# Decays one chunk ahead in four buffers, a pad ahead of the projections' input, and matmuls of 512 + 256 columns

## The chip, the cores and the metric

The kernel runs on one core of a Trainium2 chip. The metric is the time of one execution on the device in microseconds, the median of several runs. TensorE multiplies matrices, VectorE (DVE), ScalarE (ACT) and GpSimd (POOL) work element by element, SyncE (SP) issues loads. Each has a queue of its own, in which instructions run in their order; semaphores tie the queues together. SBUF is the memory on the core with 128 partitions, PSUM holds the results of matmuls.

## The reference

One encoder block over 1024 tokens of width 1024: a combined projection, a gated DeltaNet of 4 heads (convolution, decay, chunks, both directions), an mLSTM of 4 heads, an output projection, and PEER, which picks 16 of 128 x 128 single-neuron experts for each token and head. Cut to what the change touches:

```python
p = _rmsnorm(x, norm1_g[l]) @ w_in[l]          # (gq, gk, gv, gz, ga, gb, mq, mk, mv, mo, mi, mf)
qkv = silu(_conv_centred(concat([gq, gk, gv]), conv_w))
qh, kh = _l2norm(q) * DK ** -0.5, _l2norm(k)
# chunked delta rule, per direction
g = jnp.cumsum(g, axis=-1)
decay = jnp.exp(jnp.where(incl, g[..., :, None] - g[..., None, :], -jnp.inf))
a_mat = jnp.where(strict, jnp.einsum("bhncd,bhnsd->bhncs", k_beta, k) * decay, 0.0)
t_mat = lax.linalg.triangular_solve(eye + a_mat, eye, left_side=True, lower=True)
qk = jnp.where(incl, jnp.einsum("bhncd,bhnsd->bhncs", q, k) * decay, 0.0)
...
x = x + concat([y_a, y_b], -1) @ w_out[l]
h2 = _rmsnorm(x, norm2_g[l])
scores = jnp.einsum("thpd,hpkd->thpk", h2 @ w_q, sub_keys)        # router: queries, then keys
act = jax.nn.gelu(jnp.einsum("td,thkd->thk", tb, u_tab[idx]), approximate=False)
x = x + jnp.einsum("thk,thkd->td", gate * act, v_tab[idx])
```

## The kernel before

The program is one stream of about 47,700 instructions in five stages. The front part (0 to about 530 us) normalises, projects and prepares both mixers; the triangular levels, the delta rule and the mLSTM follow to 735; the output projection to 860; then the router and the experts' activations to about 2300, and the experts' output to the end.

**Projections.** `hTh` and `hTl` are the normalised input, transposed, as a high and a low part in a format for fast matmuls (fp32r); each weight is split alike (`split_w`: load `wraw`, high part `whi` by a cast on ScalarE at L120, low part `wlo` by a subtraction on GpSimd at L121). `mm3` (L128) adds three products (high-high, high-low, low-high) over 8 slices: one group of 24 matmuls makes 128 output columns for 512 tokens in a PSUM tile `psP`, of which there are four. 66 such groups, 1584 matmuls, make the whole projection.

**Convolution.** `conv_tile` (L400) projects one of 8 key/query tiles, convolves it on VectorE and applies Silu on ScalarE. The loop behind it takes each tile in two halves: transposes (`psR`), Square, sum and Sqrt for the norm, product, transposes back (`psB`, L440), and a copy by ScalarE into `kT` or `qT` (L441); there are 16 such copies.

**Decay stage.** `amat(n)` handles chunk n of 8 in both directions d, so there are 16 units. It multiplies keys with keys (`pkk`, L452) and keys with queries (`pqk`, L455). A unit loads two tiles of 256 KB, repeated for all partitions, on SyncE's queue (`dec` and `bb`, L387); GpSimd adds a mask (L459); four Exps follow on ScalarE (L462); GpSimd multiplies (L463); VectorE multiplies `bb` by `pkk` (L464) and `dec` by `pqk` (L469). ScalarE's queue issues six stores: `atsc` (L465), four small `dinv` (L468) and `qksc` (L470). `dec` and `bb` have three buffers each (`APB`) in a pool `ap` on the right side of SBUF. `invert` (L480) reads `dinv` of four chunks and inverts 32 x 32 blocks on VectorE in 31 steps.

**mLSTM keys and queries.** 16 groups of projections fill `mkT` and `mqT` (L513 to L520); ScalarE copies them out of `psP`. Their pool `mp` is opened behind the decay stage's in the text. Then come values and gates (`plain`, `value_rows`), 24 groups more.

**Order.** A scheduler arranges the instructions on each engine by its own timeline; the order of the text is the priority. A tile that takes the place of an older one waits for all that used it. `tc.issue_after(ins)` keeps the instructions inside it behind `ins`.

**Experts.** `act_steps` (L1087) multiplies 128 experts' rows by 768 tokens (`TB`), twice 384 columns (`HB`), with the same three products over 8 slices; there are 128 tiles, 6144 matmuls. The router's queries (psq) take `w` = 384 columns in the same manner.

Of the kernel before, what the change touches and what calls it, by code (L numbers as in the profile page):

```python
# [8 lines left out]
F32 = mybir.dt.float32  # L9
# [5 lines left out]
AF = mybir.ActivationFunctionType  # L15
OP = mybir.AluOpType
PSUM = bass.MemoryType.PSUM

P = 128
# [3 lines left out]
NT = S // P  # L23
NH = 4
# [18 lines left out]
GRING, KRING, RING = 6, 4, 6  # L43
WB, VX = 8, 2
LAG = 8
APB = 3
NBUF = 3
AHEAD = 1
EPS = 1e-6
# [13 lines left out]
def kernel(ctx, tc, x, norm1_g, w_in, conv_w, gdn_a_log, gdn_dt_bias, gdn_norm_g,  # L63
# [85 lines left out]

    st_c = ExitStack()  # L150
    csp = pool(st_c, "csp", side="right")
    negm = csp.tile([P, 2, P], F32, name="negm")
    lvl = csp.tile([P, 2, 2, P // 2], F32, name="lvl")
    ones = csp.tile([P, P], F32, name="ones")
# [238 lines left out]
    def unit(d, h, n):  # L393
        return d * 32 + h * NT + n
# [21 lines left out]
    def to_rows(cv, q):  # L416
# [2 lines left out]
            T.transpose(ps[:, j], cv[:, (4 * q + j) * P:(4 * q + j + 1) * P], ident)  # L419
        return ps  # L420

    for ty, dst in ((1, kT), (0, qT)):
        for h in range(NH):
            cv = conv_tile(ty * NH + h)
            for q in range(2):
                ps = to_rows(cv, q)
                rows = wx.tile([P, 4, P], F32, name="rows", bufs=2)
                A.activation(rows, ps, AF.Square)
                ss = wp.tile([P, 4], F32, name="ss", bufs=2)
                V.tensor_reduce(ss, rows, axis=AX, op=OP.add)  # L430
                A.activation(ss, ss, AF.Sqrt, bias=epsc)
                V.reciprocal(ss, ss)
                if ty == 0:
                    V.tensor_scalar(ss, ss, HD ** -0.5, None, op0=OP.mult)
                V.tensor_tensor(rows, ps, ss[:, :, None].to_broadcast([P, 4, P]), op=OP.mult)
                if ty == 1:
                    dmas(ksc[4 * q:4 * q + 4, :, h].rearrange("n p e -> p n e"), rows)
                pb = px.tile([P, 4, P], F32, name="psB", tag="px")
                for j in range(4):
                    T.transpose(pb[:, j], rows[:, j], ident)  # L440
                A.copy(dst[:, h, q * 512:(q + 1) * 512].rearrange("p (a b) -> p a b", b=P), pb)  # L441


    st_b = ExitStack()
    ap_ = pool(st_b, "ap", side="right")
    HALF = NT // 2

    def amat(n):
        cs = slice(n * P, n * P + P)
        pkk = px.tile([P, NH, P], F32, name="pkk", tag="px")  # L450
        for h in range(NH):
            T.matmul(pkk[:, h], kT[:, h, cs], kT[:, h, cs], start=True, stop=True)  # L452
        pqk = px.tile([P, NH, P], F32, name="pqk", tag="px")
        for h in range(NH):
            T.matmul(pqk[:, h], kT[:, h, cs], qT[:, h, cs], start=True, stop=True)  # L455
        for d in range(2):
            dec = rows_bcast(ap_, 0, d, n, "dec", bufs=APB)
            bb = rows_bcast(ap_, 1, d, n, "bb", bufs=APB)
            G.tensor_tensor(dec, dec, negm[:, d:d + 1].to_broadcast([P, NH, P]), op=OP.add)  # L459
            for h in range(NH):  # L460
                u = unit(d, h, n)
                A.activation(dec[:, h], dec[:, h], AF.Exp, bias=gcol[:, J_NG, u:u + 1])  # L462
            G.tensor_tensor(bb, dec, bb, op=OP.mult)  # L463
            V.tensor_tensor(bb, pkk, bb, op=OP.mult)  # L464
            dmas(atsc[d, n], bb)  # L465
            for b in range(4):
                sl = slice(32 * b, 32 * b + 32)
                dmas(dinv[d, n, :, b].rearrange("h s c -> s h c"), bb[sl, :, sl])  # L468
            V.tensor_tensor(dec, pqk, dec, op=OP.mult)  # L469
            dmas(qksc[d, n], dec)  # L470


# [27 lines left out]
        dmas(blocks_of(yinv, 0, half), Y[fw].rearrange("p s c -> p (s c)"))  # L500
        dmas(blocks_of(yinv, 1, half), pq[bw])

    for half in range(2):
        for n in range(half * HALF, half * HALF + HALF):
            amat(n)
        invert(half)
    st_b.close()
    st_a.close()

# [266 lines left out]

    h2sc = scratch("h2sc", [S, D])
    TB = NB * P
    HB = TB // 2
    pg = pool(ctx, "pg")  # L780
    h2Th = pg.tile([P, KD, TB], F32R, name="h2Th")
    h2Tl = pg.tile([P, KD, TB], F32R, name="h2Tl")
# [96 lines left out]
    def router_topk(blocks, hh, hl, between, gate, keep):  # L879
# [6 lines left out]
        off_c = wo.tile([P, TOPK, n], BF16, name="off_c")  # L886
        dof_c = wo.tile([P, TOPK, n], BF16, name="dof_c")
        io_c = wo.tile([P, TOPK, n], BF16, name="io_c")
        nh = 2 if nt > 512 else 1
        w = nt // nh  # L890

        def top16(src, m, vv, ii):
            V.max(vv[:, 0:8], src)
# [6 lines left out]
        def scores(h):  # L900
            sc = wo.tile([P, nb, 2, NK], F32, name="sc", bufs=1)
            for p in range(2):
# [3 lines left out]
                kyT = wo.tile([P, NK], F32, name="kyT", bufs=2)  # L906
                dma(kyT, keys[hp])
                qy = wo.tile([P, nt], F32, name="qy", bufs=2)
                for half in range(nh):
                    ps = psK.tile([P, 512], F32, name="psq")  # L910
                    sl = slice(half * w, half * w + w)
                    mm3(ps[:, :w], lambda k: wh[:, k], lambda k: wl[:, k],
                        lambda k: hh[:, k, sl], lambda k: hl[:, k, sl], KD)
                    A.copy(qy[:, sl], ps[:, :w])
# [165 lines left out]

    def act_steps(uh, ul, psA):

        pa = psA.tile([P, 2, 512], F32, name="pa")
        for k in range(KD):
            for m, (a, b) in enumerate(((uh, h2Th), (uh, h2Tl), (ul, h2Th))):
                for half in range(2):
                    T.matmul(pa[:, half, :HB], a[:, k], b[:, k, half * HB:half * HB + HB],  # L1087
                             start=(k == 0 and m == 0), stop=(k == KD - 1 and m == 2))
            if k < KD - 1:
                yield None  # L1090
        ge = de.tile([P, TB], F32, name="ge", bufs=2)
        A.activation(ge.rearrange("p (a b) -> p a b", b=HB), pa[:, :, :HB], AF.Gelu)
        yield ge

    def act_tile(uh, ul, psA):
# [258 lines left out]
```

## Time and profile before

| | us |
|---|---|
| median of 3 runs | 3323.37 (3322.82 to 3323.91) |
| the profiled execution | 3328.18 |
| its span | 3326.4 |
| TensorE busy | 3170.6 (95% of the span) |
| VectorE busy | 2250.3 |
| GpSimd busy | 1611.2 |
| ScalarE busy | 1224.3 |
| mean granted TensorE clock | 0.977 of full speed |

The profiled execution's own time lies 4.8 us above the median, 0.14%. A row of the chain of waits is the piece of work that ended last at its time; a row of a timeline is an instruction or a run of equal ones, and in brackets the idle time ahead of it and who ended it. "PE" is TensorE. A small unlabelled "q" behind an engine (ACTq) is its queue issuing a transfer.

### The profile page before, as it was taken

How to read it: one execution, taken by the hardware profiler on the slowest of the kernel's cores; microseconds unless marked ns; L12 is line 12 of the kernel's file. 1: busy time of each engine (PE TensorE's matmuls, PEld its weight loads, DVE VectorE, ACT ScalarE, POOL GpSimd, SP SyncE). 2: the span in 40 equal slices, each digit the busy share in tenths (PEclk: the TensorE clock that was granted, in tenths of full speed). 3: DMA queues.
4: the chain of work that ended last, by engine and by line, in shares of the span. 5: the costliest groups of instructions: out<-in, count | busy, mean ns of one | idle time of the engine just before them, and what ended most of it. 6: DMA issues, size and time to landing. Idle time of an engine off the chain costs nothing.

```text
span 3326.4 us, 47752 instructions
## 1 busy us (share of the span) xinstructions
PE 3170.6 (95%) x17106; PEld 2883.3 (87%) x17106; DVE 2250.3 (68%) x5058; ACT 1224.3 (37%) x2223; POOL 1611.2 (48%) x1187
## 2 busy tenths in 40 slices
PE   7798789989999999989999999998999999999998
PEld 6686678987899999989999999996888888888887
DVE  5441682576667767866666666667888775988784
ACT  5443433324323233436566566542222122221211
POOL 1223323442088888886666666643443331453340
PEclk9898999999999999999999999999999999999999
DMA  3216635877545445657988988889999876998882
GB/s 102 71 51 146 172 91 182 250 224 239 176 92 103 85 93 109 144 131 249 316 277 294 320 292 289 310 288 374 355 326 322 306 273 213 372 339 314 283 298 98
DMA packets 486398, 745.86 MB, mean 224 GB/s; under 512 B 106928, under 2 KB 328560, under 8 KB 485392
## 3 DMA queue, kind: packets, MB, share of 16 engines
q1 hardware_dynamic: 279152, 335.68, 32.0%
q0 software_dynamic: 129024, 268.69, 26.8%
q10 hardware_dynamic: 77984, 138.43, 11.3%
q8 instruction: 135, 2.21, 0.3%
q14 instruction: 103, 0.84, 0.1%
HBM read 603.82 MB, written 138.84 MB: 223 GB/s over the span
## 4 chain that ended last, share of the span: by engine, by line
PE 79%; DMA 8%; DVE 7%; issue 2%; ACT 2%; POOL 1%; ACTq 0%; SPq 0%; DVEq 0%; POOLq 0%
PE pa L1087 29%; PE po L1282 15%; PE held L1282 15%; PE psq L128 5%; PE psP L128 5%; PE psg L1208 3%; PE psO L128 2%; DVE pq L496 1%; DMA dinv<-bb 1%; DVE cv L411 1%; PE pss L920 1%; DMA Wt<-rowb 1%; DMA dec<-rowb 1%; DVE Yd L498 1%; DMA qksc<-dec 1%
## 5 line engine op out<-in xcount | busy, mean ns | idle before, releaser
L1121 POOL DMA_INDIRECT gd<-gateB,idxB x384 | 646.9, 1685 | 194.4 <-issue 111.9
L1022 POOL DMA_INDIRECT g<-in_peer_v_dram,idxA x256 | 352.8, 1378 | 515.2 <-DVE ac L1047 375.1
L1087 PE MATMUL pa<-h2Th,uh 128*128 128x384 f32 x2048 | 557.8, 353 | 0.0
L1087 PE MATMUL pa<-h2Th,ul 128*128 128x384 f32 x2048 | 525.9, 337 | 0.2 <-DVE ul L1078 0.2
L1087 PE MATMUL pa<-h2Tl,uh 128*128 128x384 f32 x2048 | 523.6, 336 | 0.0
L1022 POOL DMA_INDIRECT g<-in_peer_u_dram,idxA x256 | 350.6, 1370 | 332.7 <-DVE act L1031 266.1
L1087 PEld LDWEIGHTS pa<-h2Th,ul 128*128 128x128 f32 x2048 | 372.0, 188 | 0.5 <-DVE ul L1078 0.5
L1087 PEld LDWEIGHTS pa<-h2Tl,uh 128*128 128x128 f32 x2048 | 370.9, 188 | 0.0
L1252 ACT CAST wh<-g 128x768 fp32r<-128x768 f32 x128 | 106.7, 834 | 689.6 <-PE po L1282 599.0
L1087 PEld LDWEIGHTS pa<-h2Th,uh 128*128 128x128 f32 x2048 | 349.1, 190 | 0.0
L1047 DVE SCALAR_TENSOR_TENSOR ac<-g,act,ac 128x1024 f32<-128x1024 f32 x254 | 324.6, 1278 | 6.9 <-DMA g<-in_peer_v_dram,idxA 5.6
L1031 DVE CUSTOM_DVE_ANT_0 g<-g,h2A 128x1024 f32<-128x1024 f32 x256 | 305.6, 1218 | 21.1 <-DMA g<-in_peer_u_dram,idxA 21.1
L1203 DVE TENSOR_SCALAR at<-iotr,iT,gT 128x128 f32<-128x128 f32 x384 | 133.0, 365 | 220.4 <-PE psg L1208 220.2
L1282 PE MATMUL held<-h2Tl,wh 128*128 128x512 f32 x576 | 223.0, 389 | 1.5 <-DVE h2Tl L1261 1.5
L1282 PE MATMUL po<-h2Th,wh 128*128 128x512 f32 x576 | 224.1, 389 | 0.0
L1282 PE MATMUL po<-h2Tl,wh 128*128 128x512 f32 x576 | 224.1, 389 | 0.0
L1282 PE MATMUL po<-h2Th,wl 128*128 128x512 f32 x576 | 224.1, 389 | 0.0
L1282 PE MATMUL held<-h2Th,wl 128*128 128x512 f32 x576 | 222.0, 389 | 0.0
L1282 PE MATMUL held<-h2Th,wh 128*128 128x512 f32 x576 | 219.8, 389 | 0.9 <-ACT h2Th L1260 0.9
L1077 ACT CAST uh<-g 128x1024 fp32r<-128x1024 f32 x128 | 134.3, 1049 | 215.1 <-PE pa L1087 212.9
L1291 DVE TENSOR_TENSOR oacc<-po,oacc 128x512 f32<-128x512 f32 x186 | 127.4, 685 | 124.8 <-PE po L1282 124.4
L128 PE MATMUL psP<-hTh,whi 128*128 128x512 f32 x512 | 206.8, 404 | 2.5 <-ACT whi L120 2.5
(389 smaller groups left out, 6710.6 us busy)
## 6 DMA issues: line engine op xcount, KB each, us to landing
g<-in_u_t_dram SPq DMA_DIRECT2D x128, 512.0 KB
g<-in_peer_v_dram SPq DMA_DIRECT2D x128, 512.0 KB
gesc<-ge ACTq DMA_DIRECT2D x128, 384.0 KB
g<-gesc SPq DMA_DIRECT2D x128, 384.0 KB
gd<-zero ACTq DMA_DIRECT2D x24, 1024.0 KB
go<-stage ACTq DMA_DIRECT2D x6, 4096.0 KB
gt<-go SPq DMA_DIRECT2D x64, 384.0 KB
gt<-gd SPq DMA_DIRECT2D x192, 128.0 KB
```

Source lines behind the costliest of these rows:

```text
L128: T.matmul(ps, a(i), b(i), start=(k == 0), stop=(k == 3 * nk - 1))
L1022: tc.keep_in_program_order(G.indirect_dma_start(out=g, out_offset=None, in_=tab, in_offset=bass.IndirectOffsetOnAxis(ap=idxA[:, b, k // TO ...
L1031: V.tensor_tensor_reduce(out=g, in0=g, in1=h2A, op0=OP.mult, op1=OP.add, scale=1.0, scalar=0.0, accum_out=acts[b][:, k:k + 1])
L1047: V.scalar_tensor_tensor(accs[b], g, w, accs[b], op0=OP.mult, op1=OP.add)
L1077: last_act.append(A.copy(uh, ur).ins)
L1087: T.matmul(pa[:, half, :HB], a[:, k], b[:, k, half * HB:half * HB + HB], start=(k == 0 and m == 0), stop=(k == KD - 1 and m == 2))
L1121: tc.keep_in_program_order(G.indirect_dma_start(out=gd[b], out_offset=bass.IndirectOffsetOnAxis(ap=idxB[:, b, h, k:k + 1], axis=0), in_=ga ...
L1203: V.tensor_scalar(at, iotr, iT[:, t:t + 1], gT[:, t:t + 1], op0=OP.is_equal, op1=OP.mult)
L1208: mms.append(T.matmul(ps[:, j], bt, at, start=True, stop=True).ins)
L1252: last_act.append(A.copy(wh, ge).ins)
L1282: T.matmul(po, a[:, tl], b[:, cl], start=(m == 0 and (q == 0 or not mine)), stop=(m == last and (q == NG - 1 or not mine)))
L1291: V.tensor_tensor(dst, po, dst, op=OP.add)
```

## The change

Three things change.

1. **A pad.** `csp.tile([P, 48])` takes 192 bytes of each partition ahead of the other tiles of that side. The built programs place `hTh` at byte 158144 before and 157952 after, `hTl` at 190912 and 190720: before 192 bytes past a multiple of 256, now on one. The other tiles that TensorE reads as its moving operand stand on such multiples in both.
2. **The decay stage.** Loads, mask, Exps and GpSimd's product go into `decays(n)`, which is called one chunk ahead of `amat(n, decs)`. `dec` and `bb` have four buffers. The Exps stand behind the twelfth of the 16 copies into `kT`/`qT`. VectorE makes all four products of a chunk before the stores are issued.
3. **Columns.** The 768 tokens of an act tile, and of the router's queries, are cut into 512 + 256 instead of 384 + 384. The number of matmuls stays.

```diff
-APB = 3
+APB = 4
...
     csp = pool(st_c, "csp", side="right")
+    csp.tile([P, 48], F32, name="pad")
...
+    laid = []
...
-                A.copy(dst[:, h, q * 512:(q + 1) * 512].rearrange("p (a b) -> p a b", b=P), pb)
+                laid.append(A.copy(dst[:, h, q * 512:(q + 1) * 512].rearrange("p (a b) -> p a b", b=P), pb).ins)
...
-    def amat(n):
+    def decays(n):
+
+        out = []
+        for d in range(2):
+            dec = rows_bcast(ap_, 0, d, n, "dec", bufs=APB)
+            bb = rows_bcast(ap_, 1, d, n, "bb", bufs=APB)
+            G.tensor_tensor(dec, dec, negm[:, d:d + 1].to_broadcast([P, NH, P]), op=OP.add)
+            with tc.issue_after(laid[11]):
+                for h in range(NH):
+                    u = unit(d, h, n)
+                    A.activation(dec[:, h], dec[:, h], AF.Exp, bias=gcol[:, J_NG, u:u + 1])
+            G.tensor_tensor(bb, dec, bb, op=OP.mult)
+            out.append((dec, bb))
+        return out
+
+    def amat(n, decs):
...
-            G.tensor_tensor(bb, dec, bb, op=OP.mult)
+        for dec, bb in decs:
             V.tensor_tensor(bb, pkk, bb, op=OP.mult)
+            V.tensor_tensor(dec, pqk, dec, op=OP.mult)
+        for d, (dec, bb) in enumerate(decs):
             dmas(atsc[d, n], bb)
...
-            V.tensor_tensor(dec, pqk, dec, op=OP.mult)
             dmas(qksc[d, n], dec)
...
-    for half in range(2):
-        for n in range(half * HALF, half * HALF + HALF):
-            amat(n)
-        invert(half)
+    ready = decays(0)
+    for n in range(NT):
+        decs = ready
+        if n + 1 < NT:
+            ready = decays(n + 1)
+        amat(n, decs)
+        if n % HALF == HALF - 1:
+            invert(n // HALF)
...
-    HB = TB // 2
+    PARTS = [slice(c, min(c + 512, TB)) for c in range(0, TB, 512)]
...
-        pa = psA.tile([P, 2, 512], F32, name="pa")
+        pa = psA.tile([P, 1024], F32, name="pa")
...
-                for half in range(2):
-                    T.matmul(pa[:, half, :HB], a[:, k], b[:, k, half * HB:half * HB + HB],
+                for sl in PARTS:
+                    T.matmul(pa[:, sl], a[:, k], b[:, k, sl],
```

Lines of the changed kernel are one higher from L151 on, and fifteen higher behind the decay stage.

The pool `ap` fills its side of SBUF downwards. Its lowest buffer begins at byte 84352 of a partition before, at 80064 now (a buffer each of `dec` and `bb`, 2048 bytes, and the pad less). `mkT` takes bytes 67328 to 83712 in both, so two buffers of `dec` now lie on its place.

The scheduler's order on ScalarE, before, among the convolution's copies (`rows` and `ss` belong to the norm of one half, `whi` is the high part of a weight):

```order
L520 ACTIVATE mkT_1888<-psP_1895 128x512 [waits PE_49]
L441 COPY kT_403<-psB_921 128x512 [waits PE_49]
L428 ACTIVATE rows_932<-psR_927 128x512 [waits DMAHW0_49,PE_49]
L431 ACTIVATE ss_934<-ss_934,epsc_59 128x4 [waits DVE_49]
L120 CAST whi_2007<-wraw_2005 128x1024 [waits DMAHW7_49,PE_49,Pool_49]
L520 ACTIVATE mkT_1888<-psP_1921 128x512 [waits PE_49]
```

And now, at the end of the decay stage (`qksc` is the last store of the last unit, `DMAHW1` the lane that reports its landing):

```order
L480 DMA dinv<-bb_1750 32x4x32 [waits DMAHW0_49]
L481 DMA qksc<-dec_1748 128x512 [waits DMAHW1_49,DVE_49]
L535 ACTIVATE mkT_1889<-psP_1896 128x512 [waits DMAHW1_49]
L535 ACTIVATE mkT_1889<-psP_1922 128x512
L535 ACTIVATE mkT_1889<-psP_1954 128x512
L535 ACTIVATE mkT_1889<-psP_1980 128x512
L535 ACTIVATE mkT_1889<-psP_2012 128x512 [waits PE_49]
```

The first copy into `mkT` stood ahead of half of the copies into `kT`; it now stands behind the last store of the stage, with the copies of all four `psP` tiles in a row.

On TensorE, before, in the decay stage (a piece of a group of projections, a chunk's two products, the next piece):

```order
L128 MATMUL psP_2421<-hTh_130,whi_2416 128x512 [waits Activation_49]
L128 MATMUL psP_2421<-hTl_131,whi_2416 128x512
L128 MATMUL psP_2447<-hTh_130,whi_2416 128x512
L128 MATMUL psP_2447<-hTl_131,whi_2416 128x512
L452 MATMUL pkk_1506<-kT_403 128x128 [waits DVE_49,PE_49]
L452 MATMUL pkk_1506<-kT_403 128x128 x3
L455 MATMUL pqk_1511<-qT_402,kT_403 128x128 [waits DVE_49,PE_49]
L455 MATMUL pqk_1511<-qT_402,kT_403 128x128 x3
L128 MATMUL psP_2421<-hTh_130,wlo_2417 128x512 [waits Pool_49]
```

And now, over the stage's last two chunks (the six chunks before stand right ahead of them in the same manner):

```order
L469 MATMUL pkk_1758<-kT_404 128x128 [waits DVE_49,PE_49]
L469 MATMUL pkk_1758<-kT_404 128x128 x3
L472 MATMUL pqk_1763<-qT_403,kT_404 128x128 [waits DVE_49,PE_49]
L472 MATMUL pqk_1763<-qT_403,kT_404 128x128 x3
L469 MATMUL pkk_1784<-kT_404 128x128 [waits DVE_49,PE_49]
L469 MATMUL pkk_1784<-kT_404 128x128 x3
L472 MATMUL pqk_1789<-qT_403,kT_404 128x128 [waits DVE_49,PE_49]
L472 MATMUL pqk_1789<-qT_403,kT_404 128x128 x3
L128 MATMUL psP_2012<-hTh_131,whi_2008 128x512 [waits Activation_49]
L128 MATMUL psP_2012<-hTl_132,whi_2008 128x512
L128 MATMUL psP_2012<-hTh_131,wlo_2009 128x512 [waits Pool_49]
```

No projection stands between the chunks' products any more; 528 of the 1584 stand ahead of the first `pkk` (811 before), and the fifth `psP` tile comes behind the last chunk. Ahead of the first `pkk` there are, behind the last of those 528, only the transposes of seven halves of the convolution.

On GpSimd, before, at the first units (`negm` is the mask):

```order
L459 TENSOR_TENSOR dec_1378<-dec_1378,negm_69 128x512 [waits DMAHW3_49,DMAHW4_49,DMAHW2_49,DMAHW5_49,DMAHW0_49,DVE_49]
L459 TENSOR_TENSOR dec_1396<-dec_1396,negm_69 128x512 [waits DMAHW7_49,DMAHW3_49]
L463 TENSOR_TENSOR bb_1380<-dec_1378,bb_1380 128x512 [waits DVE_49,DMAHW2_49,Activation_49,Pool_49]
L459 TENSOR_TENSOR dec_1424<-dec_1424,negm_69 128x512 [waits DMAHW6_49,DMAHW5_49]
L463 TENSOR_TENSOR bb_1398<-dec_1396,bb_1398 128x512 [waits DVE_49,DMAHW4_49,PE_49,DMAHW6_49,Activation_49,Pool_49]
L121 TENSOR_TENSOR wlo_1053<-wraw_1050,whi_1052 128x1024 [waits DMAHW1_49,PE_49,Activation_49]
```

And now:

```order
L456 TENSOR_TENSOR dec_1369<-dec_1369,negm_70 128x512 [waits DMAHW0_49,DVE_49]
L456 TENSOR_TENSOR dec_1379<-dec_1379,negm_70 128x512 [waits DMAHW4_49,DMAHW5_49,DMAHW3_49,DMAHW6_49,DMAHW2_49,DVE_49]
L456 TENSOR_TENSOR dec_1389<-dec_1389,negm_70 128x512 [waits DMAHW5_49]
L456 TENSOR_TENSOR dec_1399<-dec_1399,negm_70 128x512 [waits DMAHW0_49]
L121 TENSOR_TENSOR wlo_1054<-wraw_1051,whi_1053 128x1024 [waits DMAHW1_49,PE_49,Activation_49]
```

Four additions instead of three stand ahead of the sixth weight tile's low part, and the products `bb` have moved behind it (they follow four weight tiles later).

## Rows read from the trace of the kernel before

**Rows 1.** Table of stretches: busy time (and instructions) of each engine.

```profile
core 0: us, PE busy (x) PEld busy (x) DVE busy (x) ACT busy (x) POOL busy (x), PEclk, DMA share, GB/s
20.00:130.00 110.00, 83.34 (x350) 66.42 (x350) 44.79 (x76) 47.50 (x81) 22.87 (x12) 0.88 0.29 67
...
262.00:400.00 138.00, 105.09 (x491) 86.70 (x491) 61.26 (x93) 56.63 (x97) 51.18 (x33) 0.88 0.69 166
400.00:530.00 130.00, 118.55 (x564) 97.88 (x562) 81.14 (x99) 39.99 (x56) 30.38 (x23) 0.96 0.39 108
...
860.00:2305.00 1445.00, 1414.19 (x8498) 1404.06 (x8498) 994.58 (x3170) 667.05 (x1328) 995.50 (x693) 0.99 0.72 217
2305.00:3326.00 1021.00, 1010.64 (x4458) 836.25 (x4456) 802.96 (x1015) 222.12 (x266) 358.07 (x252) 1.00 0.82 293
```

**Rows 2.** Chain of waits, 90 to 262 us: start, us, what.

```profile
98.20 5.79 DMA dec<-rowb
...
104.12 1.29 POOL dec L459
...
117.75 2.16 POOL dec L459
...
126.94 1.12 PE psB L440 x4
...
137.44 0.44 PE psB L440 x4
...
215.50 12.15 PE psP L128 x53
```

**Rows 3.** Waits, 262 to 400 us: total us, times, longest.

```profile
DVE bb L464 <- POOL bb L463: 68.4, 9, 19.9
POOL dec L459 <- DMA dec<-rowb: 48.0, 6, 20.5
```

**Rows 4.** Chain of waits at the end of the projections.

```profile
523.25 5.36 PE psP L128 x23
```

**Rows 5.** Chain of waits of the whole span: output projection, act tile, router queries.

```profile
805.28 10.90 PE psO L128 x48
...
940.80 29.15 PE pa L1087 x168
...
1361.23 5.75 PE psq L128 x48
```

**Rows 6.** Timeline of GpSimd, 84 to 131 us.

```profile
121.64 2.34 POOL L121 TENSOR_TENSOR wlo<-wraw,whi 128x1024 fp32r<-128x1024 f32 x1 [0.51 <-ACT whi L120]
```

**Rows 7.** Timeline of VectorE: the sum in one half of the convolution.

```profile
254.79 0.69 DVE L430 TENSOR_REDUCE ss<-rows 128x4 f32<-128x512 f32 x1 [6.39 <-ACT rows L428]
```

**Rows 8.** Timeline of ScalarE: the copy of the same half.

```profile
262.12 0.59 ACT L441 COPY qT<-psB 128x512 f32<-128x512 f32 x1 [4.19 <-PE psB L440]
```

**Rows 9.** Chain of waits of the whole span, 262 to 320 us.

```profile
274.84 2.40 DMA dinv<-bb
...
294.54 8.98 DMA atsc<-bb
...
313.45 9.09 DMA dec<-rowb
```

**Rows 10.** SyncE's DMA queue, 314 to 322 us: packets, MB, share of 16 engines.

```profile
q1 hardware_dynamic: 1122, 0.56, 78.7%
```

**Rows 11.** Timeline of ScalarE, 262 to 300 us.

```profile
264.18 1.92 ACTq L468 DMA_DIRECT2D dinv<-bb  x4
...
270.08 5.14 ACTq L468 DMA_DIRECT2D dinv<-bb  x4
...
277.44 1.28 ACT L462 ACTIVATE dec<-dec,gcol 128x128 f32<-128x128 f32 x4
```

**Rows 12.** Timeline of VectorE: products of the first two units and the last.

```profile
263.08 1.29 DVE L464 TENSOR_TENSOR bb<-pkk,bb 128x512 f32<-128x512 f32 x2 [6.06 <-PE pkk L452]
...
394.21 0.69 DVE L464 TENSOR_TENSOR bb<-pkk,bb 128x512 f32<-128x512 f32 x1
```

More of the change, by code (lines that the diff above doesn't have):

```diff
@@ L455, in amat @@
             T.matmul(pqk[:, h], kT[:, h, cs], qT[:, h, cs], start=True, stop=True)
[L456 to L462, printed above, removed]
-            G.tensor_tensor(bb, dec, bb, op=OP.mult)
+        for dec, bb in decs:
             V.tensor_tensor(bb, pkk, bb, op=OP.mult)
+            V.tensor_tensor(dec, pqk, dec, op=OP.mult)
+        for d, (dec, bb) in enumerate(decs):
             dmas(atsc[d, n], bb)
@@ L888, in router_topk @@
         io_c = wo.tile([P, TOPK, n], BF16, name="io_c")
-        nh = 2 if nt > 512 else 1
-        w = nt // nh
         def top16(src, m, vv, ii):
@@ L908, in scores @@
                 qy = wo.tile([P, nt], F32, name="qy", bufs=2)
-                for half in range(nh):
+                for c in range(0, nt, 512):
                     ps = psK.tile([P, 512], F32, name="psq")
-                    sl = slice(half * w, half * w + w)
+                    w = min(512, nt - c)
+                    sl = slice(c, c + w)
                     mm3(ps[:, :w], lambda k: wh[:, k], lambda k: wl[:, k],
@@ L1091, in act_steps @@
         ge = de.tile([P, TB], F32, name="ge", bufs=2)
-        A.activation(ge.rearrange("p (a b) -> p a b", b=HB), pa[:, :, :HB], AF.Gelu)
+        A.activation(ge, pa[:, :TB], AF.Gelu)
         yield ge
```

## The prediction

> **What bounds the kernel now.** I read the table of stretches first. From 860 us to the end TensorE is busy 2424.8 of 2466 us, so time can be won there only by matmuls that themselves get shorter. The front part has the gaps: 27 us from 20 to 130, 33 us in the decay stage (262 to 400) and 11 us after it [rows 1]. Then I read the chain of waits around those gaps. Before 130 it runs through three loads of `dec`, VectorE's and GpSimd's small work and the Exps; TensorE starts again at 126.94, at the lower of its two clock levels (four transposes 1.12 us, against 0.44 us ten microseconds later) [rows 2]. From there to 262 the chain is TensorE's alone, runs of projections with eight transposes between two of them: no gap. In the decay stage the view of waits says who is late: VectorE's products wait 68 us for GpSimd's `bb`, GpSimd waits 48 us for loads of `dec` [rows 3]. TensorE loses only 33 us there because the scheduler has put pieces of projections between the `pkk`/`pqk` matmuls, as the rows of the order before show. So the loads set the pace of the decay stage, and projections hide most of it. The last projection ends at 528.6, then the triangular levels begin [rows 4].
>
> **The change, part by part.**
>
> **Columns.** 48 matmuls of 384 columns take 8.3 us by the row of 168 in 29.15 us, 173.5 ns each; 48 of 256 take 5.75 us, 119.8 ns each; 48 of 512 from aligned tiles 10.90 us, 227.1 ns each [rows 5]. A pair costs 347.0 ns now and 346.9 ns then. There are 3456 pairs (3072 in act tiles, 384 in the router's queries): at 0.1 ns a pair 0.3 us, and if each width had a further nanosecond, 3 us either way. I take 0.
>
> **Alignment.** The pad moves `hTh`/`hTl` only. 53 projections took 12.15 us, 229.2 ns each, 2.1 ns more than the aligned 512 [rows 2, 5]. There are 1584 projections: 3.3 us if the address is the reason, 0 if not. I take 227 ns below.
>
> **The Exps behind the twelfth copy.** They leave ScalarE's queue at 105 to 122. But each GpSimd queue entry counts too: before, the third add of `dec` ran at 117.75 and the low half of the next weight tile (`wlo`) at 121.64 [rows 6]; after, four adds stand ahead of that `wlo` (rows of the order on POOL). The first and the third add began at 104.12 and 117.75 [rows 2], 6.8 us from one load to the next, so the fourth comes between 117.75 and 124.6; at 122, add 1.3 for the add and 2.3 for `wlo`: TensorE goes on at about 125.7 instead of 126.9. Gain 1 us; 14 us if the adds were not in the way (a rival, below).
>
> **Four buffers.** This decides. With a fourth pair, the pool reaches 4096 bytes further down and lies over the place of `mkT`. The first copy into `mkT` must wait until every unit of the decay stage has let go: it stands right behind the last store on ScalarE and waits for that store's lane, where before it stood among the conv copies. Four projections can be finished (four PSUM buffers), the fifth waits for the copy. So TensorE has 528 projections, 22 groups of 24, ahead of the first `pkk` (811 before), and then only `pkk`/`pqk` until the last store has landed. 44 groups, 1056 matmuls, come behind. What the projections hid lies open.
>
> **The sum.** (1) From 125.7 to the last projection of the fourth group: 239 projections at 0.227 = 54.3, 57 transposes at 0.11 = 6.3, restart 1: **187**. (2) Behind them stand the transposes of seven conv halves, each a chain: Square 0.60, sum 0.69, Sqrt 0.30, reciprocal and scale 0.35, product 0.69, two groups of transposes 0.88, copy 0.59 and handovers, some 4.5 us; in the rows, from a sum at 254.79 to the end of its copy at 262.71, it took 7.9, with TensorE busy elsewhere in between [rows 7, 8]. Seven times 4.5 is 31.5; 16 Exps (1.28 for four) and three table loads of 1.28 add 9: last copy at **228**, bounds 218 (the additions hidden) and 243 (7.9 each). (3) The first four units are loaded and made; `pkk`, `pqk` and eight products of 0.65 bring **235**. (4) Twelve units remain. Each needs two loads whose buffers come free only when the stores of four units before have landed. A load took 5.79 us, another 9.09 [rows 2, 9], and in 8 us with little else on it the queue moved 1122 packets, 140 a microsecond [rows 10]; a load is 512 packets of 512 bytes, 3.65 us, a unit 7.3. On ScalarE a unit is 2.7 us of issues (1.92 for four small stores and two more like them), up to 6 when the lanes are held (5.14 for the four), and 1.28 of Exps [rows 11]: 4.0 to 7.4. The pace before was 15 units in 131 us, 8.7 (products at 263.08 and 394.21 [rows 12]). I take 7.3, the nearest to both loads and ScalarE; ends 4.0 and 8.7. 12 x 7.3 = 88: **323**. The block inversion of the first half shares VectorE with the last six units; I let its steps lie in the waits for loads. (5) Issue of the last stores 2.7, landing 9 (8.98 [rows 9]), the copy 0.6, in all 12.3: projections go on at **336**. (6) 1056 x 0.227 = 239.7, 112 transposes and level matmuls at 0.11 = 12.3, restart at half clock 1.5 and 3 for gaps (11 in the 130 us of before): 256, so the levels begin at **592** instead of 528.6, 63 us later. Nothing behind can make that good, since TensorE is the bound there and its order stays. The profiled execution is 4.8 us over the median; I carry the difference to the median: 3323.4 + 63 = **3386**.
>
> **A rule weighed.** The loads took 5.8 to 9.1 us, and the queue's packets set their pace. The Trainium skill, "DMA: Bandwidth & Descriptors", section "Anatomy of one DMA — SWDGE (gpsimd) path", gives 2.0 us plus bytes by 436 GB/s for a DMA of that path: by that an estimate of 2.6 us for 256 KB, and the loads would not bind. By that rule the sum would have ScalarE's 4.0 us a unit, and 296 in place of 336 (the shorter rival below). The trace disagrees by a factor of two to three, on a queue of another kind, with sources that are repeated for all partitions; I go by the rows.
>
> **The rivals.**
> *Faster: the queues are quick when nothing else is on them.* With no more than ScalarE's issues in a unit (2.7 us), the last copy at 218 and a landing of 2.4 us at the end (one of the small stores took that [rows 9]), the twelve units run from 225 to 257, the projections go on at 263, and the levels begin at 263 + 256 = 519, 9.6 us earlier: 3314. The point from which it decides: projections back before 272.6 (528.6 - 256). For it: four units made ahead, and no weight loads on the queue in the stage. Against: 6 to 9 us a load in these rows.
> *Slower than forecast: the pace of before stays.* 8.7 us a unit and the last copy at 243: 250 + 104 + 12 = 366, +93: 3417. For it: the round trip from a store to the next load is as long as before, and the inversion's steps stand ahead of the last products.
> *Shorter.* 4.0 us a unit with the last copy at 228: 235 + 48 + 13 = 296, +23: 3347. For it: ScalarE has no copies and casts to do in between.
> *The change does not do what it says, or does more:* the early gap stays (in my sum), or vanishes, because the fourth load comes early: 12 us off, 3374. That alters the size only.
>
> **How the numbers follow.** Forecast (+30 to +90) 0.75; shorter, +7 to +30, 0.11; longer, over +90, 0.05; faster 0.06; the same, where a fast block and the later restart cancel, 0.03. A measurement of this kernel tells about 0.2% from no change, 6.6 us. The range, 3350 to 3418, runs from the shorter case's time to the longer one's and leaves out a little under two in ten.
>
> **What the profile of after would show.** TensorE busy without a break to about 187, then small pieces, then nothing but `pkk`/`pqk` until about 336; idle of `psP` ended by ScalarE's copy into `mkT`, and that by the last store. `psI` at about 592. Loads still 6 to 9 us. Act tiles: 512 at 227 ns, 256 at 120 ns, the stretch from 860 to 3326 as long as now. I am wrong if the projections go on before 273, if `mkT` is copied during the stage, or if the act tiles change by more than 3 us.

## The result

| | before | after |
|---|---|---|
| median | 3323.1 us | 3412.8 us (3410.6 to 3414.3) |
| span of the profiled execution | 3326.4 | 3411.0 |
| TensorE busy | 3170.6 | 3168.7 |
| mean granted TensorE clock | 0.977 | 0.964 |

The changed kernel takes 1.0265 times as long (95% interval 1.0252 to 1.0279), 89.7 us more. The forecast was 3386 (+63) in a range of 3350 to 3418. The place was the forecast one; most of its terms were too small. That the sum still fell inside the range is partly luck, as the section on the prediction says. By the spans of the two profiled executions, from which the lengths below are read, the loss is 84.6 us, since that of the kernel before lay 4.8 above its median.

### The profile page after: what moved, and what is told of

The parts are those of the page before. It is cut to its first block, busy times and chain, and to the rows that moved or that the text cites. A ratio compares the mean times of both kernels' runs of the same rounds, so it can differ in the third digit from the quotient of the medians.

```text
span 3411.0 us, 47753 instructions
## 1 busy us (share of the span) xinstructions
PE 3168.7 (93%) x17106; PEld 2733.2 (80%) x17106; DVE 2254.0 (66%) x5058; ACT 1210.0 (35%) x2209; POOL 1603.9 (47%) x1187
## 4 chain that ended last, share of the span: by engine, by line
PE 52%; DMA 1%; DVE 0%; ACT 0%; issue 0%; SPq 0%; ACTq 0%; DVEq 0%
PE pa L1102 20%; PE po L1297 15%; PE held L1297 14%; PE psg L1223 2%; DMA g<-gesc 1%; DMA g<-in_peer_v_dram 0%; DMA gesc<-ge 0%; DVE oacc L1030 0%; ACT g L1027 0%; DVE g L1264 0%; DVE g L1046 0%; DVE ac L1062 0%; DVE v L1276 0%; DVE g L1030 0%; DVE h2Tl L1276 0%
## 5 line engine op out<-in xcount | busy, mean ns | idle before, releaser
L1102 PE MATMUL pa<-h2Th,uh 128*128 128x512 f32 (+1 forms) x2048 | 559.0, 354 | 1.0 <-ACT uh L1092 1.0
L1102 PE MATMUL pa<-h2Th,ul 128*128 128x512 f32 (+1 forms) x2048 | 527.8, 339 | 0.3 <-DVE ul L1093 0.3
L1102 PE MATMUL pa<-h2Tl,uh 128*128 128x512 f32 (+1 forms) x2048 | 527.1, 338 | 0.0
L1037 POOL DMA_INDIRECT g<-in_peer_u_dram,idxA x256 | 350.7, 1370 | 329.2 <-DVE act L1046 263.0
L1102 PEld LDWEIGHTS pa<-h2Th,ul 128*128 128x128 f32 x2048 | 313.6, 189 | 45.1 <-DVE ul L1093 0.6
L1102 PEld LDWEIGHTS pa<-h2Tl,uh 128*128 128x128 f32 x2048 | 314.0, 189 | 43.3
L1102 PEld LDWEIGHTS pa<-h2Th,uh 128*128 128x128 f32 x2048 | 312.6, 190 | 27.7 <-ACT uh L1092 1.2
L121 POOL TENSOR_TENSOR wlo<-wraw,whi 128x1024 fp32r<-128x1024 f32 x32 | 80.1, 2507 | 313.1 <-ACT whi L120 313.1
L128 PE MATMUL psP<-hTh,wlo 128*128 128x512 f32 x512 | 205.4, 401 | 15.0 <-POOL wlo L121 15.0
```

The source lines that it names most:

```text
L121: (G if name == "w" else V).tensor_tensor(lo, raw, hi.bitcast(F32), op=OP.subtract)
L128: T.matmul(ps, a(i), b(i), start=(k == 0), stop=(k == 3 * nk - 1))
L1037: tc.keep_in_program_order(G.indirect_dma_start(out=g, out_offset=None, in_=tab, in_offset=bass.IndirectOffsetOnAxis(ap=idxA[:, b, k // TO ...
L1102: T.matmul(pa[:, sl], a[:, k], b[:, k, sl], start=(k == 0 and m == 0), stop=(k == KD - 1 and m == 2))
```

## The profile after

The table of stretches, with the columns of [rows 1]:

```profile
20.00:130.00 110.00, 85.48 (x361) 68.42 (x360) 46.05 (x79) 45.13 (x73) 22.32 (x11) 0.89 0.33 75
130.00:190.00 60.00, 54.60 (x252) 44.84 (x252) 29.58 (x34) 25.84 (x37) 10.30 (x4) 0.94 0.26 66
190.00:262.00 72.00, 27.41 (x153) 23.62 (x151) 27.45 (x46) 27.96 (x49) 9.20 (x6) 0.65 0.13 36
262.00:400.00 138.00, 53.07 (x223) 45.09 (x224) 68.00 (x115) 23.52 (x61) 37.74 (x26) 0.64 0.47 119
400.00:530.00 130.00, 123.63 (x548) 100.93 (x547) 40.12 (x41) 31.96 (x44) 28.45 (x23) 0.97 0.30 83
530.00:630.00 100.00, 100.00 (x497) 83.68 (x495) 33.95 (x28) 32.86 (x46) 20.55 (x11) 1.00 0.33 98
```

TensorE does the same work, but between 190 and 400 us it is busy for 80 of 210. The projections that used to lie there run from 400 to 630, where TensorE is full. What it waits for, from 20 to 640 us (total, times, longest):

```profile
PE pkk L469 <- DVE bb L474: 59.7, 4, 27.7
PE psB L442 <- DVE rows L437: 35.4, 8, 13.1
PE psP L128 <- ACT mkT L535: 34.9, 1, 34.9
PE psP L128 <- POOL wlo L121: 15.0, 2, 11.5
...
PE psP L128 <- ACT xp L406: 4.9, 1, 4.9
```

Of the five, the first three belong to the time in which no projection is at hand: the chunks' products wait for PSUM buffers that VectorE has not yet read, the last halves of the convolution wait for each other, and the first projection behind the stage waits for the copy into `mkT`. The end of that wait, on ScalarE and then on TensorE (timelines, as in [rows 11] for the kernel before):

```profile
357.16 1.95 ACTq L480 DMA_DIRECT2D dinv<-bb  x4
359.20 0.39 ACTq L481 DMA_DIRECT2D qksc<-dec  x1
361.29 2.07 ACT L535 ACTIVATE mkT<-psP 128x512 f32<-128x512 f32 x4 [7.62 <-DVE Yd L509]
```

```profile
361.94 0.80 PE L128 MATMUL psP<-hTh,whi 128*128 128x512 f32 x1 [34.90 <-ACT mkT L535]
```

The last store is issued at 359.20, four copies follow at 361.29 in one piece (the four full `psP` tiles), and TensorE goes on 0.65 us later. The releaser in brackets, VectorE, is not the one: the order names the lane of the last store as what the first copy waits for, and the view has put the wait down to an event near it. A run further down (e11, whose stage is shorter) has the same copies, again 2.1 us behind the issue of the last store, and there the view names that store:

```profile
315.89 2.06 ACT L535 ACTIVATE mkT<-psP 128x512 f32<-128x512 f32 x4 [7.91 <-DMA qksc<-dec]
```

The first matmul of L594, in the levels, stands at 632.2 (530.7 before):

```profile
L594 PE MATMUL psI<-X,AT x224: 221/275/324, 632.2 to 825.9; 128*128 128x64 f32 x112
```

## The experiments

Each of the twelve kernels (e1 to e12) was timed beside the kernel before on one chip, but not all on the same chip. The median of the kernel before lay between 3314.6 and 3325.9 us, so the ratios are what is compared, and microseconds lost or gained are worked out from the ratios. "Projections in the stage" counts, in the order, those between the first and the last `pkk`.

| kernel | projections in the stage | ratio to before (95%) |
|---|---|---|
| before | 224 | 1 |
| before, four buffers (e2) | 0 | 1.0307 (1.0291 to 1.0322) |
| after | 0 | 1.0265 (1.0252 to 1.0279) |
| after, pool above `mkT`, Exps not held (e6) | 53 | 1.0113 (1.0096 to 1.0130) |
| after, pool above `mkT` (e1) | 89 | 1.0086 (1.0070 to 1.0101) |
| before, four buffers above `mkT` (e7) | 170 | 1.0019 (1.0010 to 1.0029) |
| after, three buffers, Exps not held (e10) | 221 | 0.9986 (0.9977 to 0.9994) |
| after, three buffers (e5) | 209 | 0.9961 (0.9947 to 0.9975) |
| before, columns and held Exps (e9) | 242 | 0.9957 (0.9945 to 0.9969) |
| the same, sixth low part on VectorE (e12) | 247 | 0.9941 (0.9927 to 0.9955) |

### Is it the overlap with mkT?

e2 is the kernel before with one number changed:

```diff
-APB = 3
+APB = 4
```

> The kernel before with four buffers of dec and bb and nothing else. Overlap theory: 528 projections ahead of the first pkk and none between the chunks' products, an idle TensorE until the last store has landed, 3390 to 3425 us. Rival (the new order of the decays is the cause, four buffers are harmless): 3315 to 3326 us.

3426.8 us, 1.0307. The overlap alone makes it slower than the whole change does. Its waits of TensorE (100 to 640 us) are those of after:

```profile
PE pkk L452 <- DVE bb L464: 67.7, 3, 27.3
PE psB L440 <- DVE rows L435: 44.5, 8, 15.6
PE psP L128 <- ACT mkT L520: 28.9, 1, 28.9
```

e1 is the other half: the change with all of its parts, and the 4096 bytes of `y_id` given back, so that the pool ends 448 bytes above `mkT`. The identity that `y_id` held is made anew by an iota on GpSimd, 1.1 us for each of the two inversions; no run has that edit alone.

```diff
-    y_id = dp.tile([P, 32, 32], F32, name="y_id")
-    G.iota(y_id, pattern=[[1, 32], [-1, 32]], base=0, channel_multiplier=0, ...)
-    V.tensor_scalar(y_id, y_id, 0.0, None, op0=OP.is_equal)
...
-        V.tensor_copy(Y, y_id)
+        G.iota(Y, pattern=[[1, 32], [-1, 32]], base=0, channel_multiplier=0, ...)
+        V.tensor_scalar(Y, Y, 0.0, None, op0=OP.is_equal)
```

> The changed kernel with all of its parts, but without the tile y_id (the identity is made afresh in Yd for each half), so that the pool of dec and bb, with four buffers, ends 448 bytes above mkT. Overlap theory (the wait of the first mkT copy for the whole decay stage is what costs): no projection waits for an mkT copy, projections stand between the chunks' products again (823 ahead of the first pkk, against 528), the levels begin at 530 us or before, and the time is 3300 to 3325 us. Rival (calling the decays one chunk ahead, with its stores behind both products, is slow by itself, since loads and stores wait for each other's lanes): the stage keeps some 9 us a unit and the time stays above 3360 us.

3354.7 us, 1.0086, between the two expectations. The wait for `mkT` is gone and with it 1.8% (59 us), but 29 us over the kernel before remain. So neither theory had the whole. The waits of TensorE, 100 to 640 us, and ScalarE's timeline at the end of the stage:

```profile
PE pkk L469 <- DVE bb L474: 42.4, 4, 16.2
PE psP L128 <- ACT whi L120: 37.4, 1, 37.4
```

```profile
380.04 0.39 ACTq L481 DMA_DIRECT2D qksc<-dec  x1
380.46 1.28 ACT L547 ACT_TABLE_LOAD   x1 [5.95 <-DMA dinv<-bb]
381.75 2.07 ACT L547 ACTIVATE cv<-psP 128x512 f32<-128x512 f32 x4
383.68 2.01 ACT L120 CAST whi<-wraw 128x1024 fp32r<-128x1024 f32 x2
```

TensorE now waits for weights. The scheduler has put no cast of a weight (`whi`) between the first and the last store of the stage on ScalarE's queue; in the kernel before there are seven. Again the projections stand behind the last store, this time by the order alone, with no data to wait for.

### How many projections are left for the stage?

From this came a theory with numbers: what counts is how many projections the order leaves inside the stage. e7 gives the kernel before four buffers above `mkT` (the edits of e2 and e1), e5 sets `APB = 3` in the changed kernel, e6 is e1 with the `issue_after` around the Exps taken away.

> The kernel before with four buffers and without the tile y_id, so that the pool ends above mkT; the decays are made where they were. 170 projections between the first and the last pkk: by the theory of the projections 54 x 0.229 = 12 us lost, 3330 to 3342 us. Rival (four buffers without the overlap help, since a unit has a longer way round the ring): 3320 us and less.

3322.6 us where before took 3314.6: 1.0019, by the ratio 6 us lost (by the medians 8) for 12 expected. Four buffers gain nothing even where they do no harm to `mkT`.

> As the changed kernel with the pool above mkT, and the Exps not held behind the twelfth copy. It has 50 projections between the first and the last pkk: by the theory of the projections 174 x 0.229 = 40 us lost, 7 gained, 3350 to 3365 us. Rival (holding the Exps back is what costs): 3330 us and less.

3353.7 us, 1.0113, 38 us where 33 were expected (40 lost, 7 gained); the run has 53 projections in the stage, not 50. Holding the Exps back is not what costs.

> The changed kernel with three buffers of dec and bb instead of four, all else as changed. Theory after the first runs: what counts is how many projections the order leaves between the first and the last pkk, where TensorE would otherwise wait for the decay stage; the kernel before has 224 there, the one with four buffers above mkT had 89 and was 30 us slower (37 with the columns' gain taken off), which is 135 projections of 0.229 us, 31 us. This one has 209, so 15 x 0.229 = 3 us lost and 7 gained by the columns: 3315 to 3327 us. Rival (the decays one chunk ahead, the Exps behind the twelfth copy or the order of the stores cost by themselves): 3345 us and more.

3303.4 us where before took 3314.6: 0.9961. The rival falls; the theory's own figure was too high by some 10 us. With three buffers the change is 13 us faster than the kernel before.

The order of the four agrees with the count of projections, from 53 to 209. It is a count of the order, not a cause by itself: e5 with 209 is faster than before with 224 (and than e10, below, with 221), so something else gained there.

### What the parts are worth alone

e3 has the columns and nothing else, e4 the pad and nothing else.

> The kernel before with 512 + 256 columns in act tiles and router queries and nothing else. By the prediction's term (0.1 ns a pair of matmuls) 3322 to 3325 us. Rival, from the profile after, where the stretch from the first to the last act tile is 10 us shorter: 2.9 ns a pair, 3311 to 3316 us.

3317.1 us, 0.9980 (0.9971 to 0.9990): 3 to 10 us gained, between the two expectations. The pairs themselves hardly differ: 166 matmuls of an act tile take 28.78 us in a row, 346.7 ns a pair, against 347.0. In the same stretch of the two kernels, before first, then e3 (columns as in [rows 1]), TensorE is idle less:

```profile
880.00:2230.00 1350.00, 1334.99 (x8119) 1333.41 (x8118) 932.13 (x3085) 641.14 (x1297) 961.57 (x669) 0.99 0.70 206
```

```profile
880.00:2230.00 1350.00, 1338.39 (x8152) 1191.40 (x8151) 939.85 (x3086) 644.20 (x1298) 967.36 (x671) 1.00 0.71 208
```

Idle falls from 15.0 to 11.6 us, and weight loading is busy for 142 us less. 0.3 ns for 3456 pairs is 1 us. Most of the idle time is one wait in the middle of the act tiles: the first matmul of `psg` waits for `at`, which VectorE makes behind a product that waits for gathered rows of `in_peer_u_dram`. (In e8 and e9 the view names `bt`, made by ScalarE for the same matmul, as the last to come.) Here are that wait in before, in e3 and in after, and the row of VectorE that holds `at` up in before:

```profile
PE psg L1208 <- DVE at L1203: 9.9, 1, 9.9
```

```profile
PE psg L1208 <- DVE at L1203: 7.6, 1, 7.6
```

```profile
PE psg L1223 <- DVE at L1218: 1.2, 1, 1.2
```

```profile
1487.63 1.22 DVE L1031 CUSTOM_DVE_ANT_0 g<-g,h2A 128x1024 f32<-128x1024 f32 x1 [7.97 <-DMA g<-in_peer_u_dram,idxA]
```

The wait is 7.4 to 9.9 us in the four profiles without the new columns (before, e2, e4, e7). In the ten with them it is 1.2 to 2.3 us in six (after, e5, e8, e9, e10, e12) and 7.6 to 8.1 in four (e1, e3, e6, e11), whose profiled executions lie 4 to 8 us above their kernels' medians; e3's took 3324.7 us, 7.6 above. From the first to the last act tile the six with the short wait take 1370 to 1373 us, the other eight 1376 to 1381. So the 6.5 us go with this wait more than with the pairs, and the rows of e3 show little of them. Why the gather comes in time in some executions and not in others, and whether the columns are the reason, is not shown.

> The kernel before with the pad and nothing else. If the address costs the 2.1 ns a projection that the prediction carried as its upper end: 226.9 to 227.3 ns apart and 3319 to 3321 us. If it costs nothing, as the profile after suggests (228.9 ns apart): 3322 to 3324 us.

3325.7 us, 1.0005 (0.9996 to 1.0014): nothing. A run of 33 projections takes 7.57 us in both kernels. Here it is with the pad (chain of waits):

```profile
205.92 7.57 PE psP L128 x33
```

229.4 ns each, from an address on a multiple of 256. The address is not why projections take 2 ns more than the output projection's matmuls; why they do stays open.

e9 adds the held Exps to the columns, on the kernel before; e10 takes them away from e5.

```diff
+            with tc.issue_after(laid[11]):
                 for h in range(NH):
                     u = unit(d, h, n)
                     A.activation(dec[:, h], dec[:, h], AF.Exp, bias=gcol[:, J_NG, u:u + 1])
```

> The kernel before with two parts of the change: the columns, and the Exps behind the twelfth copy (decays made where they were, three buffers, no pad). Its order has 242 projections between the first and the last pkk and three additions, no product, ahead of the sixth weight tile. Theory: holding the Exps back shortens the early gap from 14 to some 6 us, as in the run with three buffers, and the columns give their 7 us: 0.9950 to 0.9965 of the time before. Rival (what that run gained beyond the columns comes from the decays made one chunk ahead): 0.9975 to 0.9985, the columns alone.

3301.0 us where before took 3316.0: 0.9957, as the theory had it.

> The changed kernel with three buffers and the Exps not held back: decays one chunk ahead, stores behind both products, columns, pad. Theory (the held Exps make the difference): the early gap of 14 us is back and the time is that of the columns alone, 0.9972 to 0.9990 of before. Rival (the decays made ahead make the difference): 0.9965 and less.

3312.0 us, 0.9986: also as expected. So of what the change gains with three buffers, 0.2% comes from the columns and 0.2 to 0.3% from the Exps; the decays one chunk ahead and the order of the stores give nothing that can be told. The early gap shows the Exps' part. TensorE's waits from 100 to 140 us, in e10, in e9 and in after:

```profile
PE psB L442 <- DVE rows L437: 13.1, 1, 13.1
```

```profile
PE psP L128 <- POOL wlo L121: 5.6, 1, 5.6
```

```profile
PE psP L128 <- POOL wlo L121: 11.5, 1, 11.5
```

With three additions ahead of the sixth `wlo` the gap is 5.6 us, with four 11.5; where the Exps are not held it is 13.1, and its end is VectorE's `rows`, as in the kernel before:

```profile
PE psB L440 <- DVE rows L435: 14.3, 1, 14.3
```

e12 is e9 with that `wlo` on VectorE (`split_w` is told the engine).

```diff
-        wh, wl = split_w(wp, w_in2, C_GQ + ct * P, P)
+        wh, wl = split_w(wp, w_in2, C_GQ + ct * P, P, eng=V if ct == 1 else None)
```

> The run with the columns and the held Exps, and the low part of the sixth weight tile made on VectorE instead of GpSimd, where it stands behind three additions that wait for loads. If those additions are what TensorE waits for between 112 and 118 us, that gap (5.6 us) goes and the time is 0.9935 to 0.9950 of before. Rival (the next weight tile's low part, behind the same additions, or the convolution takes the gap's place): 0.9950 to 0.9965, as without it.

3307.9 us where before took 3325.9: 0.9941 (0.9927 to 0.9955), the lowest ratio here. From 100 to 140 us no wait of TensorE is left, and from 100 to 540 this is all of its waits for a low part:

```profile
PE psP L128 <- POOL wlo L121: 0.6, 1, 0.6
```

Waits of transposes for `cv`, which ScalarE makes, have grown: 10.4 and 9.5 us for its two lines, where e9 has 8.2 and 4.5. So a part of the gap may have moved there, in the manner of the rival. The second line in e9 and in e12:

```profile
PE psR L419 <- ACT cv L536: 4.5, 2, 2.7
```

```profile
PE psR L419 <- ACT cv L536: 9.5, 3, 7.3
```

The interval also reaches into the rival's 0.9950 to 0.9965; that the gap is gone is shown, that the time follows by its 5 us is not settled by 0.9941 against 0.9957, the more so as the two were timed on different chips.

### What sets the pace of a unit?

In after, from the product of the fourth unit (its last ends at 250.9) to that of the sixteenth:

```profile
249.60 1.28 DVE L475 TENSOR_TENSOR dec<-pqk,dec 128x512 f32<-128x512 f32 x2
...
356.52 0.69 DVE L475 TENSOR_TENSOR dec<-pqk,dec 128x512 f32<-128x512 f32 x1
```

106 us for 12 units, 8.9 each, where I had taken 7.3. SyncE's own waits (245 to 365 us) say that loads wait for the small stores:

```profile
SPq L388 <- DMA dinv<-bb: 110.6, 16, 47.9
```

A unit's two loads and six stores take turns on eight completion lanes (`DMAHW0` to `7` in the order), so by this theory the small stores and the loads wait for each other. e8 takes the 64 small stores off those lanes.

```diff
-                dmas(dinv[d, n, :, b].rearrange("h s c -> s h c"), bb[sl, :, sl])
+                nc.gpsimd.dma_start(out=dinv[d, n, :, b].rearrange("h s c -> s h c"), in_=bb[sl, :, sl])
```

> The changed kernel, with the 64 small dinv stores issued on GpSimd's queue, and the mkT copies still behind the stage. It measures what sets the pace of a unit (8.9 us from 250 to 357 us in the profile after). Theory of the lanes (each unit's two loads and six stores take turns on eight completion lanes, so a load waits until small stores of the unit before have landed): a unit takes 5 to 6.5 us, the projections go on 25 to 45 us earlier, 3368 to 3390 us. Rival (the transfer of the loads itself, 3.65 us each by the packets, or ScalarE's queue): 7 us and more, 3395 to 3415 us.

3405.2 us, 1.0270, as slow as after: the theory of the lanes fails in its forecast. The units now come in rounds of four, whose products follow each other by 1.2 to 2.5 us; the last `bb` product stands at 340.4, so 12 units take 95 us, 7.9 each. SyncE and ScalarE:

```profile
273.13 11.13 SPq L388 DMA_DIRECT2D dec<-rowb  x4
```

```profile
354.32 0.45 ACTq L512 DMA_DIRECT2D yinv<-pq  x1
354.82 2.06 ACT L535 ACTIVATE mkT<-psP 128x512 f32<-128x512 f32 x4 [28.29 <-DVE pq L510]
```

Four loads take 11 us to be issued. The last store is issued at 341.7 and not at 359.2, but the time doesn't follow: the first inversion's stores (`yinv`) now stand ahead of the copies into `mkT`, which start at 354.8 and not at 361.3. A wait taken away, and the next in the queue put in its place. Nor does e8 clear the lanes altogether, since it has a price of its own: the small stores take GpSimd 0.55 us each, 35.0 us in all, in the queue in which its additions and products stand:

```profile
335.69 8.68 POOL L480 DMA_DIRECT2D dinv<-bb  x16 [2.07 <-DVE bb L474]
```

e11 leaves out half of the loads, and with them the betas.

```diff
-            bb = rows_bcast(ap_, 1, d, n, "bb", bufs=APB)
+            bb = ap_.tile([P, NH, P], F32, name="bb", bufs=APB)
...
-            G.tensor_tensor(bb, dec, bb, op=OP.mult)
+            G.tensor_tensor(bb, dec, dec, op=OP.mult)
```

> The changed kernel without the loads of bb: GpSimd multiplies dec by itself in their place, so the betas are left out of the block matrices. It measures what sets the pace of a unit in the stage (8.9 us, where the prediction took 7.3 from two loads of 3.65). If the loads in series set it: 12 x 3.65 = 44 us less, 3355 to 3375 us. If it is the round trip of one tile (store landed, load, addition, Exps, store): 0 to 2 us a unit, 3390 to 3413 us.

3371.9 us, 1.0167 against 1.0265 of after: 33 us less, of the 44 that loads in series would have given. From the fourth unit to the last product:

```profile
309.98 0.69 DVE L474 TENSOR_TENSOR bb<-pkk,bb 128x512 f32<-128x512 f32 x1
```

The fourth `bb` product ends at 233.7, so 12 units take 77 us, 6.4 each: a load less takes 2.5 us off 8.9. The twelve units are 29 us shorter, and the first product stands 16 us earlier (230.0), as the first loads are fewer too; by the spans 35 us of it arrive at the end (6.5 us of what is missing is the wait for `at`, 7.7 in e11 and 1.2 in after).

The packets of the loads split the rest. In after, SyncE's queue moves them from 261.7 to 266.2 and again from 268.3; between the two, only ScalarE's queue (the stores) has packets. First 261 to 267, where 1024 of the packets on SyncE's queue, q1, are the loads', then all that moves from 266.4 to 268.1 (queue: packets, MB, share of 16 engines):

```profile
q1 hardware_dynamic: 1056, 0.52, 34.6%
```

```profile
q10 hardware_dynamic: 544, 0.33, 61.9%
```

Over the twelve units of after, the 1024 packets of 512 bytes of a unit's two loads take 6.2 us on average (4.4 to 8.3) from the first to the last, and 2.2 us pass before the first of the next unit: 8.5 us from unit to unit. In e11 the 512 packets of one load take 3.6 us and 2.3 pass: 5.8. So the loads one behind another, and a pause of a little over 2 us ahead of each unit's, make up the pace; taking a load away shortens the first and leaves the pause. What the pause consists of is not shown.

## Why the prediction was right, and where it was not

The mechanism stands as forecast: the fourth buffer lies on `mkT`, the first copy waits for the last store, four PSUM tiles fill, and 1056 projections lose their cover. e2 shows it alone. But the number is in the range partly by luck. The levels come 101.5 us later where 63 were forecast; with nothing made good behind them, as the prediction had it, 3323.4 + 101.5 = 3424.9 would have stood above the range. And one of its own signs of being wrong came true: it allowed the act tiles to change by 3 us, and they changed by 10.2.

The terms, each as a length and not as a time of day:

| term of the sum | forecast | measured |
|---|---|---|
| (1) early gap to the end of the fourth group | 125.7 to 187: 61 | 126.65 to 197.4: 71 |
| (2) to the last copy | 41 | 47.4 |
| (3) the first four units | 7 | 6.1 |
| (4) twelve units | 88 | 106.3 |
| (5) tail to the next projection | 12.3 (13 with rounding) | 4.7 |
| (6) to the levels | 256 | 270.3 |
| behind the levels | 0 | -16.9 |

The measured (6) ends at the first matmul of L594; the forecast counted to the end of the last projection, by which it would be 268.1.

**(1)** was short of a wait for `xp` (4.9 us in the waits), 0.229 us a projection instead of 0.227, and a second restart at the lower clock level. **(2)** The last four halves come 5.0 us apart, and 15.0 us behind the third:

```profile
228.16 1.08 PE L442 MATMUL psB<-ident,rows 128*128 128x128 f32 x4 [13.10 <-DVE rows L437]
...
233.14 1.09 PE L442 MATMUL psB<-ident,rows 128*128 128x128 f32 x4 [3.04 <-DVE rows L437]
...
238.12 1.09 PE L442 MATMUL psB<-ident,rows 128*128 128x128 f32 x4 [3.04 <-DVE rows L437]
...
243.10 1.09 PE L442 MATMUL psB<-ident,rows 128*128 128x128 f32 x4 [3.04 <-DVE rows L437]
```

I had put the transposes at 0.44; with TensorE idle between them it works at the lower level, 1.09 us (granted clock 0.65 from 190 to 262). That I had seen this in [rows 2] and used it for one restart only was a slip, worth half a microsecond a half (5.0 for 4.5), 3.5 in all. The other is in the 15.0 us, in which ScalarE loads a table four times and makes the 16 Exps and a Silu of the convolution ahead of that half's Sqrt:

```profile
218.93 1.28 ACT L460 ACT_TABLE_LOAD   x1
220.22 3.61 ACT L460 ACTIVATE dec<-dec,gcol 128x128 f32<-128x128 f32 x12
```

From 197 to 245 us there are six such loads of 1.28 us where I had taken three. **(4)** is the largest miss, 18 us. I took two loads in series, 7.3 us, and let the stores, the additions and the Exps hide; the pace of before, 8.7, which I had as the upper end, was nearer. By the packets the two loads take 6.2, less than I took, and the pause of 2.2 ahead of each unit's loads, which I had put at nothing, is the step that fails here. **(5)** The first copy starts 2.1 us after the issue of the last store; I had taken 9 from a store that shared the queue with loads. **(6)** Projections at 0.229 (2 us), the weights' casts and low parts after the restart (6.4 us of waits), level matmuls counted too low, and the slow restart make up most of 14.

**Behind the levels** I had written that nothing could make the loss good. 16.9 us were made good: 6.7 between the levels and the output projection and 10.2 in the act tiles:

```profile
L1102 PE MATMUL pa<-h2Th,uh x2048: 274/391/737, 968.3 to 2337.6; 128*128 128x512 f32 x94, 128*128 128x256 f32 x93
```

1369.3 us against 1379.5 (872.7 to 2252.2) before. Of these 10.2 us, 8.6 are the wait for `at`, 9.9 in before and 1.2 in after, which I had not looked at. The levels, up to the output projection, take 222.2 us before, 215.5 in after and 216.7 with the pad, which has nothing to do with them. Their first 20 us differ by TensorE's clock, in before partly at the lower level, in after and with the pad at the upper (granted clock 0.66, 1.00 and 1.00, for 113, 160 and 154 matmuls):

```profile
530.00:550.00 20.00, 19.28 (x113) 19.07 (x114) 3.38 (x8) 4.58 (x9) 4.45 (x5) 0.66 0.50 144
```

```profile
632.00:652.00 20.00, 18.64 (x160) 17.99 (x160) 6.29 (x14) 8.18 (x19) 6.72 (x7) 1.00 0.71 240
```

So neither gain can be put down to the change by what was run here.

**Columns and alignment.** 0 to 3 us was said of the columns; e3 gave 3 to 10, by the wait for `at` more than by the pairs that I had costed. The pad gave nothing; that was one end of what was said, and the sum had leaned on the other (227 ns a projection).

**The rivals.** "Faster" and "shorter" would have needed a pace of 2.7 and 4.0 us a unit. Half of the loads left out still took 6.4. The nearest was "the pace of before stays", 3417.

**The rule weighed.** By the Trainium skill, "DMA: Bandwidth & Descriptors", section "Anatomy of one DMA — SWDGE (gpsimd) path", a load of this size would take an estimated 2.6 us. The trace disagrees: in e11 the packets of one load alone take 3.6 us from the first to the last. My step from the estimate to "would not bind" was wrong as well, for two loads of 2.6 us in series are 5.2, more than the 4.0 of ScalarE. That the loads do bind is shown by e11, where leaving out one of a unit's two took 2.5 us off its pace.

**What was not asked.** I costed the wait for `mkT` as the only reason for the loss. e1 shows a second beneath it: with four buffers and the decays made ahead, the scheduler leaves no weight cast inside the stage. Had the overlap been avoided, the change would still have cost 0.9%. That the scheduler believes the stage to be short is argued, not shown; the missing casts are shown.

## What to carry to other kernels

A deeper buffer has a price that is not in its own loop: look at what address it takes, and who is next to use that address. Where a slow stage is covered by another engine's work, count in the order how much of that work is left inside the stage before and after the edit; and ask the same of what feeds the work (here the weights' casts). A change of several parts can hold a good one and a bad one: two of this one's parts, without the fourth buffer, make the kernel 0.4% faster.

## What the runs showed of the hardware that I had not expected

Four transposes took 1.09 us at TensorE's lower clock level in the tail of the convolution, 0.44 at the upper, so a chain through a mostly idle TensorE is itself longer. A start address on a multiple of 256 bytes for the moving operand changed nothing (229.4 ns a matmul of 512 columns in both). The copy that waits for the last store of the stage, 256 KB, started 2.1 us after that store's issue, with no loads beside it; stores beside loads took up to 9. Two loads of 256 KB in series, each one row repeated for all partitions, took 6.2 us from the first packet to the last, one alone 3.6.
